# Four weight products of a two-block transformer kernel turned around: residual with tokens on partitions, activations stationary, 512 weight columns moving

## The chip, the cores and the metric

The kernel runs on one core of one Trainium2 chip. The metric is the device time of one execution in microseconds (us). A core has a matmul engine (PE in the rows, its weight loads PEld), a vector engine (DVE), a scalar engine (ACT), GpSimd (POOL), and DMA queues, here issued from SyncE (SP), ScalarE and GpSimd. Matmul results land in PSUM, which has eight banks of 512 float32 columns on 128 partitions.

## What is computed

256 tokens of 2048 channels go through two blocks, all in float32.

```python
# first block
h = rmsnorm(x, attn_norm)
proj = h @ w_in                      # 2048 x 5376: queries, keys, values of branches a, b, c
mix = concat(rmsnorm(out_a), rmsnorm(out_b), rmsnorm(out_c))   # three kinds of attention
x = x + mix @ w_out                  # 2048 x 2048, "output"
h = rmsnorm(x, ffn_norm)
u = causal_dwconv(h @ w_up)          # 2048 x 11264
x = x + (silu(gate) * up) @ w_down   # 5632 x 2048, "down"
# second block
h = x @ w_in_2                       # branches a, b, c, m and g_merge, 4 x 2048 "gate" columns
gates = sigmoid(g_merge)
merged = sum(gates[b] * (o[b] @ w_branch[b]) for b in range(4))   # 4 x (1024 x 2048), "branch"
y = merged @ w_out_2
x = layer_norm(ALPHA * x + y)
```

## The kernel before

The weights, over 400 MB, pass once through the core. `run` (L429) works through one list of transfers, `stream`, each of 128 partitions by up to 2048 float32 columns (1 MB). Three buffers `raw` are filled from the SP queue; a buffer is filled again when the transfer three places earlier has been converted. Each transfer is used in parts of up to 1024 columns. A part is converted into two float32r tiles whose sum is exact: `h` by the scalar engine (L464), `l` by the vector engine (L478), some two parts ahead of their use. Each operand of a large product is split so, and three of the four partial products are made.

Two functions turn parts into matmuls. `t_tile` (L351) makes one tile of 128 output channels by 256 tokens: for every 128 rows of weights the 128 x 128 block `h` is loaded and the activations, high and low part side by side (512 columns), stream past it (`mm3`, L326), then `l` is loaded and the 256 high columns stream (L327). Both halves of the PSUM bank are then added: `join` (L337) by a copy (L332) and an add (L341), or `add_ps` by two adds into the residual (L347, L348). `n_group` (L375) makes 256 tokens by 512 output channels: the activations of 128 tokens are loaded and 512 weight columns stream past them, three times for each token half (L394 to L396), into two banks, one for each half.

PSUM is handed out by tags: `acc` has three banks, `sc` and `tr` two each, `po` one. `sc`, `tr` and `po` serve attention and transposes.

After each part `step` runs background work, written as generators: attention pairs, norms, splits. `need` runs steps until a result is there. So all engines' instructions stand in one order that Python fixes; each engine works off its own in that order.

The residual is `xT`, channels on partitions: 16 tiles of 128 x 256. `half1` and `half2` (L1126, L1137) add the output projection's two halves to it; `half2` multiplies the second with the norm of branch c, scales and splits for the up products (L1142 to L1165), and sums squares on GpSimd (L753, L754). `down_post` (L1248) adds the down products and splits. `gen_xn` (L1849) transposes the residual for the last step with 32 transposes (L1854). `gate_post` and `br_post` (L1865, L1873) make sigmoid and the merge tile by tile (L1879 to L1882, adds on GpSimd), into `xT`; `gen_ms` splits it. `z_post` and `gen_out` make the layer norm with tokens on partitions.

Order of the stream: memory keys and values, branches a, b, c, output (32 half tiles), up (34 tiles), down block 0, up (32), down block 1 (13 tiles), up (22), the rest of down, then the second block's projections, its gate and branch tiles in turns, and the last product.

Of the kernel before, what the change touches and what calls it, by code (L numbers as in the profile page):

```python
# [9 lines left out]
F32 = mybir.dt.float32  # L10
# [14 lines left out]
# columns of the packed per-channel parameters  # L25
# [9 lines left out]
# columns of the packed one-hot rows and bias tables  # L35
# [67 lines left out]
def _layout(a):  # L103
# [11 lines left out]
    r["wo"] = _lay_t(a["w_out"][0])  # L115
# [3 lines left out]
    for i, n in enumerate(FBLK):  # L119
        r[f"wd{i}"] = _lay_t(wd[f * 128:(f + n) * 128])  # L120
        f += n
# [8 lines left out]
    for n in ("u", "ga", "xb", "gb", "q", "kc", "vc", "ks", "kw", "gc", "qm", "gm", "gg"):  # L130
        r["w2" + n] = _lay_t(o[n])
    r["w2v"] = _lay_n(o["v"])
# [6 lines left out]
    t = [_lay_t(wb[i]) for i in range(4)]  # L139
    r["wbr"] = np.stack([np.concatenate([t[0], t[1]], 2), np.concatenate([t[2], t[3]], 2)], 1)  # L140
# [44 lines left out]
class Build:  # L185
# [5 lines left out]
    def __init__(self, tc, D, out, ctx, taps=None):  # L191
# [28 lines left out]
        self.alone = False  # L220

    # ---- allocation
# [4 lines left out]
    def take(self, i, dt):  # L227
        """half of a two-slot tile; a tile of its own for each use of both halves"""
# [60 lines left out]

    def sm(self):  # L290
# [19 lines left out]
    # ---- small instruction helpers  # L310
# [6 lines left out]
    def split(self, t, dst):  # L317
        """float32 tile -> exact sum of two float32r tiles"""
# [4 lines left out]
    def mm3(self, ps, wh, wl, x, first, last):  # L323
        """ps[:, :T] + ps[:, T:] += w^T x with both operands split; w stationary"""
# [12 lines left out]
    def join(self, ps, scale=None):  # L337
        """the two halves of a product, added"""
# [36 lines left out]
    def n_group(self, ap, xs, post):  # L375
        """out[tokens, 512] for one 512-column group; ap [nl, 128, 2048]"""
# [26 lines left out]
    def add(self, loads):  # L403
        """transfers in order, each followed by the uses of its parts"""
# [102 lines left out]
    # ---- background work  # L507
# [21 lines left out]
    def later(self, *fs):  # L529
        """one function per step, the first in this step"""  # L530
# [17 lines left out]
    def need(self, cond, what):  # L548
        """emit background work until cond() holds"""
# [16 lines left out]

    def head_norm(self, ps, gain, dest, done):
        """per-head (64 partitions) rmsnorm of a projected tile"""
# [22 lines left out]
    def bias_tile(self, dram, row, off=0):  # L591
        """tile[p, j] = f[row][p + j]; read backwards along j it is the bias of keys against queries"""
# [5 lines left out]
    def qk(self, q, k):  # L598
        """scores of two heads: [:, 0:256] second query block, [:, 256:384] first query block"""
# [9 lines left out]
    def key_pair(self):  # L609
        """keys of two heads for 128-row products, the other head's rows zero"""  # L610
# [5 lines left out]
    def key_swap(self, lo, hi, ka, kb):  # L616
        """lo holds a head in its low rows, hi another in its high rows: each into the other half too"""
# [3 lines left out]
    def to_pt(self, P1, P0):  # L621
        """P [query, key] of two heads -> transposed: key block 0 per head [128, 256], key block 1 both heads"""
# [13 lines left out]
    def pv(self, po, pt, v, first, last=True):  # L636
        """po[64 per head, T] += v^T P^T; v(hh, block) -> [128, 64]"""
# [8 lines left out]
    def softmax_a(self, s, bias, P1, P0, sm, sink=None):  # L646
        """P = exp(s + bias - max); sm columns (block, head): 0:4 minus max, 4:8 denominators"""
# [32 lines left out]
    def soft_pair(self, q, k, v, bias_src, rows, done, sink=None, sinkn=None):  # L680
        """two heads of causal softmax attention with a bias by distance; the output replaces q"""
# [75 lines left out]
    def pipe(self, n, *fs):  # L757
        """steps of a software pipeline: stage j handles item i at step i + j"""
# [6 lines left out]
    def group_norm(self, tiles, sq, g0, ys):  # L765
        """rmsnorm over a group's channels, result split into ys"""
# [23 lines left out]
    # ---- the kernel  # L790
    def setup(self):
# [4 lines left out]
        self.xT = self.cp.tile([128, 16, T], F32, name="xT")  # L796
        nc.scalar.preload_act_table_set("natural_log_exp_and_others")
# [5 lines left out]
        # work for the array until the data is here, so that its clock is up by then  # L803
# [16 lines left out]
    def tables(self):  # L820
        """distance -> bias, per head, to DRAM"""
# [64 lines left out]
    def lazy(self, lst, n, what, then=None):  # L886
        """sequence that asks for its n items when first used"""
# [9 lines left out]
    def block1(self):  # L897
        nc, D = self.nc, self.D
        V, A, G = nc.vector, nc.scalar, nc.gpsimd
        # memory keys and values  # L900
# [56 lines left out]
        # branch A  # L957
# [23 lines left out]
        def c_done(o, j):  # L981
            """group C: split with the gain, the common factor comes after the product"""
            g = self.col("gmix", 8 + j)

            def f():
# [6 lines left out]
                def f2():  # L992
# [5 lines left out]
                    def f3():  # L998
                        self.free(o)
                        if j == 7:  # L1000
                            st["rsc"] = self.slot()
                            self.rms_factor(st["sqc"], 1024, st["rsc"], self.epsc)
# [47 lines left out]
        # branches B and C  # L1050
# [54 lines left out]
        def cq_post(j):  # L1105
# [14 lines left out]
            return f  # L1120
        for j in range(8):
# [3 lines left out]
        # output projection, first the A and B halves  # L1125
        def half1(i):  # L1126
            def f(ps):
                if i == 0:
# [5 lines left out]
        sq = {}  # L1134
# [953 lines left out]
```

## Time and profile before

| | us |
|---|---|
| median of 3 runs | 2452.63 |
| lowest, highest | 2452.2, 2453.0 |
| profiled execution, span | 2453.6 |

| engine | busy us | share |
|---|---|---|
| PE | 2426.6 | 99% |
| PEld | 2096.4 | 85% |
| DVE | 1667.2 | 68% |
| ACT | 1323.6 | 54% |
| POOL | 421.6 | 17% |

The page of the profile gives busy times, the chain of work that ended last, and the costliest groups of instructions by line of the kernel. Times of single stages come from windows: the busy time of each engine between two moments, counted from the span's start, with the number of instructions that touch the window.

### The profile page before, as it was taken

Reading aid. Unit: us, or ns where it says so; the run is one execution under the profiler, and the core shown is the slowest. Engines: PE = TensorE matmul, PEld = TensorE weight load, DVE = VectorE, ACT = ScalarE, POOL = GpSimd, SP = SyncE. Lnnn points to the kernel's source line nnn. Section 1 sums busy time; section 2 is a strip of 40 time slices with the busy share of each in tenths; the row PEclk is TensorE's granted clock in tenths of the full one; section 3 lists DMA queues with packets and bytes.
Section 4 is the critical chain, followed back from the end, with each engine's and each line's share of the span. In section 5 each row is a group of like instructions: output and inputs, shape, how many; then the busy total and the mean of one; then the engine's idle time right before and its main releaser. Section 6 shows DMA issues by size and latency. Waiting matters only on the chain.

```text
span 2453.6 us, 35661 instructions
## 1 busy us (share of the span) xinstructions
PE 2426.6 (99%) x13768; PEld 2096.4 (85%) x13768; DVE 1667.2 (68%) x2662; ACT 1323.6 (54%) x2255; POOL 421.6 (17%) x470
## 2 busy tenths in 40 slices
PE   9999999999999999999999999999999999999997
PEld 8887888888888888888888888888888888888887
DVE  6768677877766777577777865757655555555566
ACT  5566566465544554455456645765554444444443
POOL 2113222532200221022003420101001111111101
PEclk9999999999999999999999999999999999999999
DMA  7554544545555555555555555445545555555553
GB/s 287 191 173 139 176 162 145 186 179 198 186 193 185 194 187 190 183 180 192 192 199 171 176 191 185 150 145 188 190 172 189 182 191 183 184 189 189 189 220 124
DMA packets 74295, 449.16 MB, mean 183 GB/s; under 512 B 8734, under 2 KB 14952, under 8 KB 25484
## 3 DMA queue, kind: packets, MB, share of 16 engines
q1 hardware_dynamic: 65052, 433.86, 50.3%
q10 hardware_dynamic: 7040, 6.29, 1.0%
q0 software_dynamic: 2032, 6.72, 0.9%
q8 instruction: 108, 1.77, 0.3%
q14 instruction: 63, 0.52, 0.1%
HBM read 442.97 MB, written 2.17 MB: 181 GB/s over the span
## 4 chain that ended last, share of the span: by engine, by line
PE 93%; DVE 4%; ACT 1%; DMA 1%; POOL 1%; issue 0%; ACTq 0%; DVEq 0%; SPq 0%; POOLq 0%
PE acc L326 51%; PE acc L327 26%; PE acc L394 3%; PE acc L396 3%; PE acc L395 3%; DVE l L478 1%; PE sc L604 1%; DVE s L315 1%; PE po L642 1%; ACT s L312 1%; PE sc L605 1%; DMA raw<-in_wmv_dram 1%; POOL s L754 0%; DMA raw<-in_wu_dram 0%; PE po L1738 0%
## 5 line engine op out<-in xcount | busy, mean ns | idle before, releaser
L326 PE MATMUL acc<-s,h 128*128 128x512 f32 x5680 | 2010.1, 398 | 2.7 <-ACT h L464 1.5
L327 PE MATMUL acc<-s,l 128*128 128x256 f32 x5680 | 1596.1, 281 | 5.0 <-DVE l L478 4.8
L326 PEld LDWEIGHTS acc<-s,h 128*128 128x128 f32 x5680 | 1067.8, 188 | 255.9 <-issue 5.2
L478 DVE TENSOR_TENSOR l<-raw,h 128x1024 fp32r<-128x1024 f32 (+1 forms) x808 | 1003.5, 1251 | 148.6 <-PE acc L327 54.6
L327 PEld LDWEIGHTS acc<-s,l 128*128 128x128 f32 x5680 | 1075.2, 189 | 10.3 <-DVE l L478 9.8
L464 ACT CAST h<-raw 128x1024 fp32r<-128x1024 f32 (+1 forms) x808 | 839.0, 1040 | 368.9 <-PE acc L326 163.5
L341 DVE TENSOR_TENSOR s<-acc,s 128x256 f32<-128x256 f32 x311 | 131.9, 424 | 397.0 <-ACT s L332 396.9
L332 ACT COPY s<-acc 128x256 f32<-128x256 f32 x319 | 118.8, 372 | 439.8 <-PE acc L327 439.8
L1882 POOL TENSOR_TENSOR xT<-xT,s 128x256 f32<-128x256 f32 x48 | 75.4, 1571 | 599.6 <-DVE s L1881 599.6
L1192 POOL TENSOR_TENSOR s<-s,s 128x256 f32<-128x256 f32 x88 | 81.9, 931 | 509.0 <-DVE s L341 509.0
L312 ACT ACTIVATE s<-s 128x256 f32<-128x256 f32 (+1 forms) x251 | 98.8, 413 | 82.8 <-DVE s L341 45.0
L394 PE MATMUL acc<-h,s 128*128 128x512 f32 x352 | 140.7, 400 | 0.9 <-ACT s L320 0.8
L396 PE MATMUL acc<-h,s 128*128 128x512 f32 x352 | 137.5, 391 | 0.2 <-DVE s L321 0.2
L395 PE MATMUL acc<-l,s 128*128 128x512 f32 x352 | 137.3, 390 | 0.0
L312 ACT ACTIVATE s<-s,sm 128x256 f32<-128x256 f32 (+1 forms) x168 | 74.3, 464 | 27.0 <-DVE sm L674 13.6
L315 DVE SCALAR_TENSOR_TENSOR s<-s,cols 128x254 f32<-128x254 f32 (+2 forms) x128 | 80.2, 627 | 6.4 <-ACT s L312 4.0
L312 ACT ACTIVATE s<-s,cols 128x256 f32<-128x256 f32 (+1 forms) x104 | 61.3, 589 | 37.2 <-POOL s L1192 23.9
L394 PEld LDWEIGHTS acc<-h,s 128*128 128x128 f32 x352 | 66.1, 188 | 15.8 <-issue 1.9
L396 PEld LDWEIGHTS acc<-h,s 128*128 128x128 f32 x352 | 66.1, 188 | 15.1 <-DVE s L321 0.7
L395 PEld LDWEIGHTS acc<-l,s 128*128 128x128 f32 x352 | 66.2, 188 | 12.8
L347 DVE TENSOR_TENSOR xT<-xT,acc 128x256 f32<-128x256 f32 x64 | 26.9, 421 | 64.8 <-PE acc L327 64.6
L315 DVE SCALAR_TENSOR_TENSOR s<-s,cols,s 128x255 f32<-128x255 f32 (+5 forms) x106 | 62.5, 592 | 3.5 <-ACT s L312 2.0
(260 smaller groups left out, 1443.1 us busy)
## 6 DMA issues: line engine op xcount, KB each, us to landing
raw<-in_wu_dram SPq DMA_DIRECT2D x88, 1024.0 KB, 4.8
raw<-in_w2gg_dram SPq DMA_DIRECT2D x64, 1024.0 KB, 4.8
raw<-in_wd_dram SPq DMA_DIRECT2D x32, 1024.0 KB, 4.8
raw<-in_wbr_dram SPq DMA_DIRECT2D x32, 1024.0 KB, 4.8
raw<-in_wc_dram SPq DMA_DIRECT2D x16, 1024.0 KB, 4.8
raw<-in_wo_dram SPq DMA_DIRECT2D x32, 512.0 KB, 3.5
raw<-in_wo_dram SPq DMA_DIRECT2D x16, 1024.0 KB, 4.8
raw<-in_wd_dram SPq DMA_DIRECT2D x16, 768.0 KB, 4.2
```

The costliest lines, as they stand in the source:

```text
L312: return self.nc.scalar.activation(out, in_, f, bias=bias, scale=scale, **k)
L315: return (eng or self.nc.vector).scalar_tensor_tensor(out, a, s, b, op0=o0, op1=o1)
L326: m(ps, lhsT=wh, rhs=x.both, start=first, stop=last, skip_group_check=True)
L327: m(ps[:, :T], lhsT=wl, rhs=x[0], start=False, stop=last, skip_group_check=True)
L332: self.nc.scalar.copy(t, ps[:, T:])
L341: self.nc.vector.tensor_add(t, ps[:, :T], t)
L394: m(ps, lhsT=xh[:, ts], rhs=h[:, s], start=k == 0, stop=False)
L395: m(ps, lhsT=xh[:, ts], rhs=l[:, s], start=False, stop=False)
L396: m(ps, lhsT=xl[:, ts], rhs=h[:, s], start=False, stop=k == nl * 4 - 1)
L464: self.nc.scalar.copy(h[:, :b - a], raws[i][:, a:b])
L478: self.nc.vector.tensor_sub(l[:, :n], raws[i][:, a:b], hl[k][:, :n].bitcast(F32))
L1192: G.tensor_mul(u, u, rs[0])
```

## The change

The residual `R` lies with tokens on partitions, in the same memory as `xT`: `res(t, a, b)` is token half t, channels a to b. Output, down, gate and branch products use `n_group` with weights laid out for it; their tiles of 128 channels become groups of 512. For down, gates, branches and the last product `banks` takes two `sc` and two `acc` banks in turn; the output projection keeps `acc`. Where the next product needs channels on partitions, `turn` makes four transposes of 128 columns, after which the scalar engine makes the high and the vector engine the low part. The residual's input is loaded once more in the new layout during branch c. The norm of branch c becomes a scalar per token. `gen_xn` goes; of the gate and branch groups the last two gates stand ahead of the last two branches.

```diff
+    def banks(self):
+        self.alt = not self.alt
+        return [self.sc(), self.sc()] if self.alt else [self.acc(), self.acc()]
+    def res(self, t, a, b):
+        return self.R[:, t * 2048 + a:t * 2048 + b]
+    def turn(self, src, post):
+        p = self.tr()
+        for c in range(2):
+            for t in range(2):
+                self.nc.tensor.transpose(p[:, c * T + t * 128:c * T + t * 128 + 128], src(t, c), self.colr("ident"))
+        return [post(c, p[:, c * T:c * T + T]) for c in range(2)]
...
-    def n_group(self, ap, xs, post):
+    def n_group(self, ap, xs, post, banks=None):
...
-                        st["ps"] = [self.acc(), self.acc()]
+                        st["ps"] = banks() if banks else [self.acc(), self.acc()]
...
+        def r_load():
+            for i in range(2):
+                nc.sync.dma_start(self.R[:, i * 2048:(i + 1) * 2048], D["xr"][:, i * 2048:(i + 1) * 2048])
+        self.hooks[len(self.stream) + 3] = r_load
...
-                self.add_ps(self.xT[:, i], ps)
+                for t in range(2):
+                    x = self.res(t, cg * 512, cg * 512 + 512)
+                    V.tensor_add(x, x, pss[t])
...
+        def half2(cg):
+            def f(pss):
                 self.need(lambda: "rsc" in st, "mix c norm")
+                junk = self.pair(F32)
+                for t in range(2):
+                    x = self.res(t, cg * 512, cg * 512 + 512)
+                    self.stt(x, pss[t], st["rsc"][:, 2 * t:2 * t + 1], x, ALU.mult, ALU.add)
+                    self.act(junk.both, x, AF.Square, accum_out=ss[:, t, cg:cg + 1])
+                self.free(*junk)
+                self.fast.append(gen_x1(cg))
...
+        def gen_x1(cg):
+            yield
+            for jj in range(2):
...
+                ps = self.turn(lambda t, c: self.res(t, (i0 + c) * 128, (i0 + c) * 128 + 128), high)
+                for c in range(2):
+                    self.stt(ys[c][1], ps[c], self.col("gffn", i0 + c), ys[c][0].bitcast(F32), ALU.mult, ALU.subtract)
+                    self.xs2.append(ys[c])
+                yield
...
-        for i in range(0, 16):
-            self.add(self.t_tile(D["wo"][i][:, :1024], YAB(), half1(i)))
+        for cg in range(4):
+            self.add(self.n_group(D["wo"][cg, :2], YAB(), half1(cg)))
...
+        def down_post(b, cg, f0, n):
+            def post(pss):
+                for t in range(2):
+                    x = self.res(t, cg * 512, cg * 512 + 512)
+                    V.tensor_add(x, x, pss[t])
                 if b == 2:
+                    self.fast.append(gen_x2(cg))
...
+            for cg in range(lo, hi):
+                self.add(self.n_group(D[f"wd{b}"][cg], Acts(f0), down_post(b, cg, f0, FBLK[b]), self.banks))
         pairs(0, 17, True)
-        down(0, 0, 16)
+        down(0, 0, 4)
         pairs(17, 33)
-        down(1, 0, 13)
+        down(1, 0, 3)
         pairs(33, 44)
-        down(1, 13, 16)
-        down(2, 0, 16)
+        down(1, 3, 4)
+        down(2, 0, 4)
...
+        def gate_post(b, cg):
+            def post(pss):
+                gt[b] = [self.pair(F32) for _ in range(2)]
                 for t in range(2):
+                    self.act(gt[b][t].both, pss[t], AF.Sigmoid)
...
+        def br_post(b, cg):
+            def post(pss):
+                g = gt.pop(b)
+                if b == 0:
+                    mt[cg] = g
+                for t in range(2):
+                    V.tensor_mul(g[t].both, pss[t], g[t].both)
+                    if b:
+                        (V if (b, cg) == (3, 3) else G).tensor_add(mt[cg][t].both, mt[cg][t].both, g[t].both)
+                        self.free(*g[t])
...
         def gen_ms():
+            for cg in range(4):
+                while cg == 3 and "merged" not in state:
                     yield
...
+                    ps = self.turn(lambda t, c: mt[cg][t].both[:, (2 * jj + c) * 128:(2 * jj + c) * 128 + 128], high)
...
+        for cg in range(4):
+            for b in range(4):
+                if (b, cg) == (2, 3):
+                    gg(2, 3)
+                    gg(3, 3)
+                    br(2, 3)
+                    br(3, 3)
+                elif (b, cg) != (3, 3):
+                    gg(b, cg)
+                    br(b, cg)
         msl = self.lazy(ms, 16, "merged")
         for cg in range(3):
-            self.add(self.n_group(D["wo2"][cg], msl, z_post(cg)))
+            self.add(self.n_group(D["wo2"][cg], msl, z_post(cg), self.banks))
```

## Rows read from the trace of the kernel before

**Rows 1.** Page, parts 1, 2, 4: busy us, granted clock, chain that ended last.

```profile
PE 2426.6 (99%) x13768; PEld 2096.4 (85%) x13768; DVE 1667.2 (68%) x2662; ACT 1323.6 (54%) x2255; POOL 421.6 (17%) x470
...
PEclk9999999999999999999999999999999999999999
...
PE 93%; DVE 4%; ACT 1%; DMA 1%; POOL 1%; issue 0%; ACTq 0%; DVEq 0%; SPq 0%; POOLq 0%
```

**Rows 2.** Page, part 5, costliest groups: busy us, mean ns, idle before, releaser.

```profile
L326 PE MATMUL acc<-s,h 128*128 128x512 f32 x5680 | 2010.1, 398 | 2.7 <-ACT h L464 1.5
...
L478 DVE TENSOR_TENSOR l<-raw,h 128x1024 fp32r<-128x1024 f32 (+1 forms) x808 | 1003.5, 1251 | 148.6 <-PE acc L327 54.6
...
L1882 POOL TENSOR_TENSOR xT<-xT,s 128x256 f32<-128x256 f32 x48 | 75.4, 1571 | 599.6 <-DVE s L1881 599.6
...
L347 DVE TENSOR_TENSOR xT<-xT,acc 128x256 f32<-128x256 f32 x64 | 26.9, 421 | 64.8 <-PE acc L327 64.6
```

**Rows 3.** Windows by stage: length, busy us (count) per engine, clock, DMA share, GB/s.

```profile
278.00:387.20 109.20, 109.20 (x659) 94.71 (x658) 79.01 (x162) 72.45 (x164) 27.61 (x38) 1.00 0.47 159
...
387.20:440.80 53.60, 53.60 (x323) 45.98 (x322) 41.26 (x87) 29.59 (x56) 7.39 (x8) 1.00 0.53 167
440.80:489.00 48.20, 46.84 (x259) 38.95 (x257) 45.28 (x71) 24.27 (x41) 30.55 (x27) 1.00 0.55 183
489.00:682.70 193.70, 191.14 (x1092) 167.91 (x1092) 151.50 (x192) 113.88 (x175) 51.00 (x54) 0.99 0.53 188
...
772.20:949.70 177.50, 177.50 (x1026) 156.51 (x1025) 136.86 (x171) 101.64 (x155) 41.52 (x46) 1.00 0.54 190
...
1803.40:2350.90 547.50, 546.61 (x3106) 474.00 (x3104) 306.29 (x386) 269.86 (x405) 74.64 (x47) 1.00 0.52 185
...
sum 248.60, PE 247.38 PEld 215.46 DVE 156.97 ACT 103.96 POOL 7.15; mean PE 82.46 PEld 71.82 DVE 52.32 ACT 34.65 POOL 2.38
```

**Rows 4.** Windows, same columns, inside the projections and inside the gates.

```profile
1700.00:1800.00 100.00, 100.00 (x579) 88.19 (x578) 62.41 (x91) 55.79 (x91) 0.00 (x0) 1.00 0.54 191
...
1900.00:2300.00 400.00, 400.00 (x2267) 346.90 (x2266) 224.90 (x284) 193.84 (x285) 55.58 (x35) 1.00 0.53 185
```

**Rows 5.** Timeline, PE: start us, duration us. An n_group, then a t_tile.

```profile
80.02 0.39 PE L394 MATMUL acc<-h,s 128*128 128x512 f32 x1
...
101.78 0.39 PE L394 MATMUL acc<-h,s 128*128 128x512 f32 x1
...
102.80 0.40 PE L326 MATMUL acc<-s,h 128*128 128x512 f32 x1
...
104.92 0.40 PE L326 MATMUL acc<-s,h 128*128 128x512 f32 x1
```

**Rows 6.** Timeline, PE: four transposes inside an n_group.

```profile
1468.13 0.39 PE L396 MATMUL acc<-h,s 128*128 128x512 f32 x1
1468.36 0.60 PE L1482 MATMUL tr<-cols,s 128*128 128x128 f32 x4
...
1469.03 0.40 PE L395 MATMUL acc<-l,s 128*128 128x512 f32 x1
...
1471.34 0.39 PE L396 MATMUL acc<-h,s 128*128 128x512 f32 x1
```

**Rows 7.** Timeline, PE: the last product's first group begins, its second begins.

```profile
2350.04 0.28 PE L327 MATMUL acc<-s,l 128*128 128x256 f32 x1
...
2352.43 0.40 PE L394 MATMUL acc<-h,s 128*128 128x512 f32 x1
...
2373.99 0.39 PE L396 MATMUL acc<-h,s 128*128 128x512 f32 x1
...
2375.64 0.39 PE L396 MATMUL acc<-h,s 128*128 128x512 f32 x1
```

**Rows 8.** Waits of PE, 380 to 500 us (total, times, longest); a window therein.

```profile
PE acc L327 <- DVE l L478: 3.9, 9, 2.3
...
494.90:498.00 3.10, 3.04 (x10) 2.67 (x11) 3.03 (x5) 2.18 (x3) 2.20 (x3) 0.53 0.00 0
```

More of the change, by code (lines that the diff above doesn't have):

```diff
@@ L138, in _layout @@
     wb = a["w_branch_2"][0]
-    t = [_lay_t(wb[i]) for i in range(4)]
-    r["wbr"] = np.stack([np.concatenate([t[0], t[1]], 2), np.concatenate([t[2], t[3]], 2)], 1)
+    r["wbr"] = np.stack([_lay_n(wb[i]) for i in range(4)])
     r["wo2"] = _lay_n(a["w_out_2"][0])
@@ L1168, in half2, with high @@
             return f
+        def gen_x1(cg):
+            yield
+            for jj in range(2):
+                i0 = 4 * cg + 2 * jj
+                ys = []
+                def high(c, p):
+                    y = self.pair()
+                    self.act(y[0], p, AF.Copy, scale=self.col("gffn", i0 + c))
+                    ys.append(y)
+                    return p
+                ps = self.turn(lambda t, c: self.res(t, (i0 + c) * 128, (i0 + c) * 128 + 128), high)
[3 more added lines that the diff above has]
+                yield
+            if cg == 3:
+                dg = self.slot()
+                V.tensor_reduce(ss2, ss, AX.X, ALU.add)
+                for t in range(2):
+                    V.tensor_scalar(dg[:, t * 128:t * 128 + 128], self.colr("ident"), ss2[:, t:t + 1], None, op0=ALU.mult)
+                yield
+                r = self.slot()
+                self.rms_rows(dg, 2048, r, self.epsc)
+                self.free(dg)
+                rs[0] = r
@@ L1175, in __getitem__ @@
                 return l[j]
-        for i in range(0, 16):
-            self.add(self.t_tile(D["wo"][i][:, :1024], YAB(), half1(i)))
+        for cg in range(4):
+            self.add(self.n_group(D["wo"][cg, :2], YAB(), half1(cg)))
         ycl = self.lazy(yc, 8, "yc")
-        for i in range(16):
-            self.add(self.t_tile(D["wo"][i][:, 1024:], ycl, half2(i)))
+        for cg in range(4):
+            self.add(self.n_group(D["wo"][cg, 2:], ycl, half2(cg)))
         xs2 = self.lazy(self.xs2, 16, "xs2")
@@ L1889, in post, with high @@
                             self.free(*y)
[L1890 to L1891 removed]
+                    for n in ("lng", "lnb"):
+                        state[n] = row_bcast(D[n], 2048)
             return post
         def gen_ms():
[L1895 to L1904 removed]
+            for cg in range(4):
+                while cg == 3 and "merged" not in state:
+                    yield
+                if cg == 3:
+                    yield
+                for jj in range(2):
+                    ys = []
+                    def high(c, p):
+                        y = self.pair()
+                        A.copy(y[0], p)
+                        ys.append(y)
+                        return p
+                    ps = self.turn(lambda t, c: mt[cg][t].both[:, (2 * jj + c) * 128:(2 * jj + c) * 128 + 128], high)
+                    for c in range(2):
+                        V.tensor_sub(ys[c][1], ps[c], ys[c][0].bitcast(F32))
+                        ms.append(ys[c])
+                    yield
+                for g in mt.pop(cg):
+                    self.free(*g)
         fst = self.cp.tile([128, 2, 8, 6], F32, name="fst")
@@ L1909, in z_tile @@
         def z_tile(j, t, ps):
-            z = xn[t, j]
-            V.tensor_add(z, ps, z)
+            z = self.res(t, j * T, j * T + T)
+            self.stt(z, z, ALPHA, ps, ALU.mult, ALU.add)
             V.bn_stats(fst[:, t, j, :], z)
@@ L1985, in block2, with gg, br @@
                 self.add(self.t_tile(D["w2" + nmn][j], x2, g_post(b, src, j)))
-        def start_xn(h, l):
-            self.slow.append(gen_xn())
-        self.start_xn = start_xn
-        first = True
-        for i in range(16):
-            for b in (0, 1, 2, 3):
-                ld = self.t_tile(D["w2gg"][16 * b + i], x2, gate_post(b, i))
-                if first:
-                    a, e, use = ld[0][1][0]
-                    def use2(h, l, use=use):
-                        self.slow.append(gen_xn())
-                        use(h, l)
-                    ld[0][1][0] = (a, e, use2)
-                    first = False
-                self.add(ld)
-                if b % 2:
-                    subs = []
-                    for k in range(2):
-                        bb = b - 1 + k
-                        xs = self.BR(self, os_[bb], bb)
-                        s = self.t_tile(D["wbr"][i, b // 2][:, k * 1024:(k + 1) * 1024], xs, br_post(bb, i))
-                        (_, [(x0, x1, u)]), = s
-                        subs.append((k * 1024, k * 1024 + 1024, u))
-                    self.add([(D["wbr"][i, b // 2], subs)])
+        def gg(b, cg):
+            self.add(self.n_group(D["w2gg"][4 * b + cg], x2, gate_post(b, cg), self.banks))
+        def br(b, cg):
+            self.add(self.n_group(D["wbr"][b, cg], self.BR(self, os_[b], b), br_post(b, cg), self.banks))
+        for cg in range(4):
+            for b in range(4):
[7 more added lines that the diff above has]
+                    br(b, cg)
         msl = self.lazy(ms, 16, "merged")
         for cg in range(3):
-            self.add(self.n_group(D["wo2"][cg], msl, z_post(cg)))
+            self.add(self.n_group(D["wo2"][cg], msl, z_post(cg), self.banks))
         kept = []
```

153 lines of the change are left out of this document (54 added, 99 removed).

## The prediction

> **What bounds the kernel now.** The page's busy shares come first: the matmul engine is busy in 2426.6 of 2453.6 us, at a granted clock of full speed in every slice, and the chain that ended last runs over it for 93% [rows 1]. Vector and scalar engine have a third and nearly half of the span free. So the time is the matmul stream's, and the question is what one weight block of 128 x 128 costs there. The costliest groups and a stretch of the matmul engine's timeline [rows 2, 5] show the two ways in which the kernel multiplies today. t_tile (L326, L327) holds a weight block and streams the activations past it: 512 columns, then 256. n_group (L394 to L396) holds activations and streams weights: per 128 rows of weights six matmuls of 512 columns for four blocks. Both move 768 columns per block, so by columns they are equal. Durations don't tell them apart (a row's 398 ns overlaps the next matmul); the spacing of starts does.
>
> In windows where only t_tile ran [rows 4], 100 us hold 579 matmuls at one place and 400 us hold 2267 at another: 345.4 and 352.9 ns per pair, thus per block. The stream has two rhythms and stays in one until something disturbs it. n_group's starts [rows 5] go from 80.02 to 101.78 us in 96 steps: 226.7 ns per matmul, or 1.5 x 226.7 = 340.0 ns per block. When a t_tile stream follows an n_group directly, it takes the slow rhythm: 102.80 to 104.92 us are six pairs, 353 ns [rows 5].
>
> **The change, part by part**, against the profiled execution (span 2453.6 us; the median of the runs is 1.0 us lower).
>
> *Matmul rate.* 2496 of the 5680 t_tile blocks become n_group's: output 256, down 44 x 16 = 704, gates and branches 1024 + 512. Their stages now take 53.6 + 48.2, 248.6 and 547.5 us [rows 3]. At 340.0 ns they would be 87.0, 239.4 and 522.2. Of the 101.8 of the output projection about 8.6 are attention matmuls, which stay (53.6 less 128 blocks at about 351 ns). I split the rest into rate (256 x 11, 704 x 12 and 1536 x 13.3 ns: 2.8 + 8.4 + 20.5 = 31.7 us) and other time that goes: about 3.3 of stalls in the second half of the output projection (48.2 less 128 x 351 ns), 0.8 in down, and 4.8 in the gates, where the 32 transposes of gen_xn sit. Together -40.6.
>
> *Stalls at stage edges.* Around 490 us the matmul engine waits 3.9 us for the converted weights of L478, once for 2.3 us, and the granted clock then is 0.53, nearly all at the lower of its two levels, 1.2 GHz, for 3 us [rows 8]. The reason is in the window 440.8 to 489: the vector engine is busy 45.28 of 48.20 us, as each block column costs it a join, a product, an add and a split beside L478 [rows 3]. The change replaces these by one operation on 512 columns per token half and column group, and transposes the result. So the first up stage, 193.7 us for 544 blocks, or 188.5 at the fast rhythm, loses 4.6 of its excess. At the last n_group, from 2350.04 to 2352.43, four matmuls take 2.4 us instead of 0.8, waiting for the last merge and split [rows 7]; the change puts eight sub-tiles of work between them. That is -1.6, and two changes of group there cost 0.3 each less with alternating banks.
>
> *Transposes added.* turn is called 8 times after each of output projection, down and merge, 24 in all, each with four 128-column transposes. Four such in an n_group stretch: twelve steps from 1468.13 to 1471.34 us take 3.21 instead of 2.72, so 0.49 each [rows 6]; 24 x 0.49 = +11.8. This counts the disturbance behind them.
>
> *Group changes.* In the last stage a new group follows from 2373.99 to 2375.64 in six steps, 1.65 instead of 1.36, for it must wait for an eviction with three accumulators and two per group: 0.3 us [rows 7]. The eight groups of the output projection keep these banks: +2.1 for seven changes. In down, gates and branches two pairs of banks alternate; a group's eviction then has a whole group, 10 to 22 us, and costs nothing. Its cover gone, 44 x 0.3 = 13 us. Entering an n_group and attention work inside one add about 1.0.
>
> *Rhythm.* The second up stage runs 177.5 us for 512 blocks, the fast rhythm [rows 3]. Behind an n_group with nothing to disturb it, I expect the slow one: 512 x 6.4 ns = +3.3. The first up stage begins among transposes; I take half of 544 x 6.4 ns, +1.7. The third is slow already.
>
> *Evictions.* An operation on 512 columns lies between the 0.42 us of L347 for 256 and the 1.25 of L478 for 1024 [rows 2]; two per group of 10.9 or 21.8 us, instead of a join each 2.8 or 5.6 us: less work than before. The merge's adds on GpSimd take 1.57 us for 256 columns [rows 2], so up to 3.1 for 512, 6.3 per branch group, beside 33 us of stream.
>
> *DMAs.* Bytes of weights are the same; the output projection's transfers grow from 512 KB to 1 MB, which doubles what three buffers hold. r_load puts 2 MB on SP's queue ahead of attention weights. There the DMA engines are busy 0.47 at 159 GB/s [rows 3]: at the rest, some 180 GB/s, 2.1 MB take 12 us, and three buffers hold 3 x 6.8 us (109.2 for 16 tiles). Nothing then; up to 6 us if the buffers were short when it is issued.
>
> *New waits.* turn's transposes wait for the residual add or the merge and stand in the matmul queue in front of the next products; the copies and splits behind them must be there before the next stage asks for its last rows. Background work is emitted once per 1024 weight columns, 2.7 us, and the last four rows of eight or sixteen come into use three such steps later. Per stage edge this costs between 0 and the 2.3 us of [rows 8], and not below 0; there are three such edges. I take 2.0 in all, nearer the free end, as the vector engine is no longer full there.
>
> The sum: -40.6 - 4.6 - 1.6 - 0.6 + 11.8 + 2.1 + 1.0 + 3.3 + 1.7 + 2.0 = -24.9. Span 2428.7, median about 2427.7, which I round to 2427.5.
>
> **The rivals.**
> - *The weight stream doesn't settle* (slower). Behind each disturbance the n_group matmuls are 231 ns apart on average for ten steps (1469.03 to 1471.34 us, [rows 6]) before they settle at 226.7. If the longer groups held a slower rhythm, as t_tile does for 400 us [rows 4], at 235 ns per matmul a block would cost the 353 ns of today and the whole 31.7 us of rate would be lost: -24.9 + 31.7 = +6.8, 2459.5. It decides at 24.9 us / 2496 / 1.5 = 6.7 ns, so from 233.3 ns per matmul on. Against it: 96 steps in a row at 226.7.
> - *Columns alone count* (no change). If both ways cost the same per column and the spacing seen were an accident of place, rate and rhythm terms go: -24.9 + 31.7 - 5.0 = +1.8, about 2454.5. Against it: the two fast figures, 345.4 and 340.0, come from undisturbed stretches. The Trainium skill has this rule (TensorE: Matmul & The Clock Gate, "Back-to-back issue gap": the isolated gap at full clock is columns / 2.4 plus 2.5 ns); an estimate by it is 325.0 against 323.7 ns per block, so some 3 us of gain in rate, less than the transposes cost. By that rule the change brings about nothing. The trace doesn't agree: 226.7 ns stand here for its 215.8.
> - *Group changes wait after all*: two banks are finished at once, and a sigmoid of both queues behind a conversion on the scalar engine. At the 0.3 us of [rows 7] for 44 groups +13, 2441.
> - *Stage edges stall*: where turn feeds the up stage, the second block and the last product, each costs what the first up stage lost now, 193.7 - 188.5 = 5.2; three of them and the 4.6 not gained, less my 2.0: +18, 2446.
> - That the change isn't what it says: the number of n_group matmuls must rise by 1.5 x 2496 = 3744. The diff leaves no doubt, so it has no chance of its own.
>
> **How the numbers follow.** Forecast 70%, with a range of its own from 2417 (both up stages fast, no waits: -5.0 - 2.0 - 3.1) to 2437 (the half of each unknown cost more). Not settling 6%, columns alone 6%, group changes 10%, stage edges 8%. The range to be right 8 times in 10 reaches from 2416 to 2446, over the forecast and the two cases of waits. About 0.2%, 4.9 us, is what a measurement here can tell from no change. Faster by more: the forecast, group changes, and half of the stage edges, 84%. Within: the other half and most of columns alone, 9%. Slower: 7%.
>
> **What would show it.** In the trace after, steps of 226.7 ns inside gate groups, a gate and branch stage near 527 us instead of 547.5, down near 244 in sum, the second up stage at 181 instead of 177.5, and no clock below full speed near 490 us. I am wrong if the steps inside long groups are 230 ns or more, if a group's first matmul waits in down or gates, or if the transposes wait for what they turn.

## The result

The changed kernel takes 2424.48 us in the median of four runs (2423.99 to 2426.03), the kernel before, timed beside it, 2452.41 (2451.93 to 2453.0): a ratio of 0.9891, 95% interval 0.9872 to 0.9910. Forecast were 2427.5 and a range of 2416 to 2446. The profiled execution has a span of 2422.8 us instead of 2453.6, so 30.8 us less; the stages are compared in these two executions.

The page of the changed kernel, parts 1 and 5 (busy us, mean ns, idle before, releaser; L345 and L346 are t_tile's matmuls now, L413 to L415 n_group's, L497 and L483 the conversions):

```profile
PE 2401.7 (99%) x12588; PEld 2037.8 (84%) x12588; DVE 1587.2 (66%) x2363; ACT 1271.9 (52%) x2071; POOL 351.4 (15%) x419
...
L497 DVE TENSOR_TENSOR l<-raw,h 128x1024 fp32r<-128x1024 f32 x800 | 1016.0, 1280 | 381.7 <-PE sc L414 193.0
...
L345 PE MATMUL acc<-s,h 128*128 128x512 f32 x3184 | 1130.3, 399 | 0.9 <-DVE s L340 0.9
...
L413 PE MATMUL acc<-h,s 128*128 128x512 f32 x864 | 341.6, 395 | 0.0
...
L413 PE MATMUL sc<-h,s 128*128 128x512 f32 x736 | 287.2, 390 | 0.0
...
L1929 POOL TENSOR_TENSOR s<-s,s 128x512 f32<-128x512 f32 x22 | 39.0, 1793 | 604.2 <-DVE s L1927 604.2
```

The pairs of L345 and L346 went from 5680 to 3184, by 2496. As in [rows 1], the matmul engine is busy from end to end, so nearly all of the gain has to be in the stream itself. The windows of the changed kernel, with the columns of [rows 3], in the order output, first, second and third up stage, the second block's projections, gates and branches, last product, tail; the last line is the sum of the three down stages:

```profile
386.40:485.30 98.90, 98.90 (x477) 80.99 (x476) 63.73 (x100) 53.87 (x96) 7.38 (x8) 1.00 0.50 175
485.30:675.40 190.10, 190.10 (x1102) 166.34 (x1101) 147.47 (x189) 113.24 (x177) 44.80 (x49) 1.00 0.54 189
762.40:943.30 180.90, 180.90 (x1025) 156.86 (x1024) 136.99 (x171) 101.56 (x155) 40.54 (x46) 1.00 0.53 186
1008.70:1133.00 124.30, 124.30 (x705) 107.80 (x704) 93.05 (x116) 69.28 (x105) 27.48 (x31) 1.00 0.53 186
1223.00:1794.80 571.80, 569.99 (x3316) 492.45 (x3316) 395.86 (x778) 337.98 (x643) 87.63 (x126) 1.00 0.51 176
1794.80:2320.40 525.60, 525.60 (x2332) 435.13 (x2332) 277.27 (x239) 225.67 (x241) 43.26 (x30) 1.00 0.55 194
2320.40:2386.20 65.80, 65.80 (x296) 54.48 (x295) 38.98 (x55) 30.23 (x48) 0.00 (x0) 1.00 0.62 228
2386.20:2422.80 36.60, 23.65 (x193) 23.06 (x191) 28.17 (x69) 5.22 (x14) 7.83 (x10) 0.87 0.16 58
...
sum 242.40, PE 242.40 PEld 200.58 DVE 135.22 ACT 101.19 POOL 7.12; mean PE 80.80 PEld 66.86 DVE 45.07 ACT 33.73 POOL 2.37
```

| stage | before | after | difference | terms of the forecast |
|---|---|---|---|---|
| up to the output product | 387.2 | 386.4 | -0.8 | 0 |
| output | 101.8 | 98.9 | -2.9 | -0.3 |
| first up stage | 193.7 | 190.1 | -3.6 | -1.9 |
| down, three stages | 248.6 | 242.4 | -6.2 | -6.3 |
| second up stage | 177.5 | 180.9 | +3.4 | +3.3 |
| third up stage | 124.3 | 124.3 | 0.0 | 0 |
| second block's projections | 570.3 | 571.8 | +1.5 | +1.0 |
| gates and branches | 547.5 | 525.6 | -21.9 | -22.4 |
| last product | 66.3 | 65.8 | -0.5 | -1.2 |
| tail | 36.4 | 36.6 | +0.2 | 0 |

(The terms are the prediction's, each turn's 0.49 us put where it lies, two of eight behind the stage that it closes, and 0.8 of the 1.0 for entries with the output. The 2.0 of new waits and the other 0.2 stood for no one stage.)

In the gates the steps between the starts of n_group's matmuls are those of [rows 5], also across a change of banks (from `acc` to `sc`). Timeline of the changed kernel, matmul engine (start us, duration us), 92 steps in 20.85 us, 226.6 ns each:

```profile
1850.10 0.39 PE L414 MATMUL acc<-l,s 128*128 128x512 f32 x1
...
1870.95 0.39 PE L413 MATMUL sc<-h,s 128*128 128x512 f32 x1
```

Why is a block cheaper so, with the same 768 columns? Where its tail begins, the changed kernel streams 256 columns at a time, 23 steps in 2.75 us, 119.6 ns each:

```profile
2386.17 0.28 PE L2092 MATMUL acc<-s,s 128*128 128x256 f32 x1
...
2388.92 0.28 PE L2094 MATMUL acc<-s,s 128*128 128x256 f32 x1
```

An estimate from these two steady figures: 256 columns more cost 107.0 ns, which leaves 12.6 ns of each matmul that don't go by columns. n_group makes 1.5 matmuls per block and t_tile two; half of 12.6 ns is 6.3, and 346.5 - 340.0 is 6.5. So the number of matmuls is enough to explain the difference from the fast rhythm, whichever operand is held. No run here holds the weights with equal lengths throughout or varies the number alone, so this is not shown. The slow rhythm's further 6.5 ns are the subject of the later experiments.

### The profile page after: what moved, and what is told of

Read it like the earlier page. It is cut to its first block, busy times and chain, and to the rows that moved or that the text cites. A ratio compares the mean times of both kernels' runs of the same rounds, so it can differ in the third digit from the quotient of the medians.

```text
span 2422.8 us, 32877 instructions
## 1 busy us (share of the span) xinstructions
PE 2401.7 (99%) x12588; PEld 2037.8 (84%) x12588; DVE 1587.2 (66%) x2363; ACT 1271.9 (52%) x2071; POOL 351.4 (15%) x419
## 4 chain that ended last, share of the span: by engine, by line
PE 94%; DVE 2%; ACT 1%; POOL 1%; DMA 1%; issue 0%; SPq 0%; ACTq 0%; DVEq 0%; POOLq 0%
PE acc L345 28%; PE acc L346 14%; PE acc L413 8%; PE acc L415 8%; PE acc L414 8%; PE sc L415 7%; PE sc L413 7%; PE sc L414 7%; PE sc L632 1%; PE po L670 1%; DVE l L497 1%; PE sc L633 1%; DMA raw<-in_wmv_dram 1%; ACT s L331 1%; PE tr L306 0%; DVE s L1390 0%
## 5 line engine op out<-in xcount | busy, mean ns | idle before, releaser
L497 DVE TENSOR_TENSOR l<-raw,h 128x1024 fp32r<-128x1024 f32 x800 | 1016.0, 1280 | 381.7 <-PE sc L414 193.0
L483 ACT CAST h<-raw 128x1024 fp32r<-128x1024 f32 x800 | 839.6, 1050 | 560.4 <-PE sc L415 244.1
L345 PE MATMUL acc<-s,h 128*128 128x512 f32 x3184 | 1130.3, 399 | 0.9 <-DVE s L340 0.9
L346 PE MATMUL acc<-s,l 128*128 128x256 f32 x3184 | 892.3, 280 | 2.0 <-DVE l L497 1.8
L345 PEld LDWEIGHTS acc<-s,h 128*128 128x128 f32 x3184 | 598.3, 188 | 143.4 <-issue 2.9
L346 PEld LDWEIGHTS acc<-s,l 128*128 128x128 f32 x3184 | 601.5, 189 | 4.6 <-DVE l L497 4.0
L413 PE MATMUL acc<-h,s 128*128 128x512 f32 x864 | 341.6, 395 | 0.0
L415 PE MATMUL acc<-h,s 128*128 128x512 f32 x864 | 336.9, 390 | 0.0
L413 PE MATMUL sc<-h,s 128*128 128x512 f32 x736 | 287.2, 390 | 0.0
L415 PE MATMUL sc<-h,s 128*128 128x512 f32 x736 | 286.5, 389 | 0.0
L414 PE MATMUL sc<-l,s 128*128 128x512 f32 x736 | 286.4, 389 | 0.0
L415 PEld LDWEIGHTS acc<-h,s 128*128 128x128 f32 x864 | 162.1, 188 | 34.8
L413 PEld LDWEIGHTS acc<-h,s 128*128 128x128 f32 x864 | 162.2, 188 | 34.0 <-issue 1.6
L415 PEld LDWEIGHTS sc<-h,s 128*128 128x128 f32 x736 | 138.1, 188 | 28.9
L413 PEld LDWEIGHTS sc<-h,s 128*128 128x128 f32 x736 | 138.2, 188 | 28.5
```

The lines of the kernel that those rows point to most:

```text
L345: m(ps, lhsT=wh, rhs=x.both, start=first, stop=last, skip_group_check=True)
L346: m(ps[:, :T], lhsT=wl, rhs=x[0], start=False, stop=last, skip_group_check=True)
L413: m(ps, lhsT=xh[:, ts], rhs=h[:, s], start=k == 0, stop=False)
L414: m(ps, lhsT=xh[:, ts], rhs=l[:, s], start=False, stop=False)
L415: m(ps, lhsT=xl[:, ts], rhs=h[:, s], start=False, stop=k == nl * 4 - 1)
L483: self.nc.scalar.copy(h[:, :b - a], raws[i][:, a:b])
```

## The experiments

Every difference below is against the changed kernel unless it says otherwise. 2424.48 us is its time, 2422.8 its span.

**Only the gates by t_tile again.** Is the gain one of rate, or of what lies beside the stream?

```diff
+                r, g = self.right(ps), gt[b][i // 2][i % 2]
+                V.tensor_add(g, ps[:, :T], r)
...
+                self.act(g, g, AF.Sigmoid)
...
-            self.add(self.n_group(D["w2gg"][4 * b + cg], x2, gate_post(b, cg), self.banks))
+            for i in range(4):
+                self.add(self.t_tile(D["w2gg"][4 * b + cg, i], x2, gate_post(b, cg, i)))
```

> The changed kernel, with only the 16 gate groups made by t_tile again (64 tiles of 128 columns, same transfers and bytes; the columns then mean other channels, so the numbers of the gates are not the reference's). Theory, the cost per block depends on which operand is held: 1024 blocks go from 340 ns to 353 (slow rhythm) or 346 (fast rhythm), so the gate and branch stage grows from 525.6 us by 13.3 or 5.5 us, and the time from 2424.5 to 2430 to 2438. Rival, columns alone count and the gain came from evictions and transposes: the stage stays within 2 us of 525.6.

It took 2437.03 us, 12.6 more. Below are the window of the gate and branch stage, 538.6 us instead of 525.6, in which 1024 blocks are t_tile's now, and the timeline inside a gate group: from 1830.13 to 1849.21 us are 54 pairs at 353.3 ns.

```profile
1793.80:2332.40 538.60, 538.60 (x2843) 460.28 (x2842) 295.54 (x302) 251.15 (x336) 43.17 (x30) 1.00 0.54 189
```

```profile
1830.13 0.40 PE L345 MATMUL acc<-s,h 128*128 128x512 f32 x1
...
1849.21 0.40 PE L345 MATMUL acc<-s,h 128*128 128x512 f32 x1
```

The matmul engine is busy in all of both stages, the DMA share is 0.54 and 0.55, and no other engine is full: the 13.0 us are the rate, 13.3 by the slow rhythm. "Columns alone count" falls.

**Three banks everywhere.** What do alternating banks save?

```diff
-        return [self.sc(), self.sc()] if self.alt else [self.acc(), self.acc()]
+        return [self.acc(), self.acc()]
```

> The changed kernel, with the three acc banks for every group instead of two pairs of banks in turn. Theory of the prediction, a change of group with three banks costs 0.3 us: 44 changes, +13 us, 2437. Rival, from the output stage of the changed kernel, whose changes with three banks show no wait: the cost depends on how soon the first bank's reader is done; down and branches (one operation of some 0.7 us on that bank) cost nothing, gates (a sigmoid) at most 0.3 us for 16 groups, so 2424 to 2430.

2424.97 us, the same. The gate and branch stage takes 525.2 us:

```profile
1794.90:2320.10 525.20, 525.20 (x2331) 434.89 (x2330) 276.92 (x238) 225.41 (x240) 43.26 (x30) 1.00 0.55 194
```

So a change of group is free there too, and the 0.3 us of [rows 7] are no price of the three banks as such. With three banks the next group needs the first bank of the last one only at its fourth matmul, 0.68 us later. Where one operation reads that bank, it is free by then. In the last product several operations read it one after the other, and there this run has the wait again at both changes, once from 2343.27 us on: two steps take 0.72 us instead of 0.45. With four banks the changed kernel has none.

```profile
2343.27 0.39 PE L415 MATMUL acc<-h,s 128*128 128x512 f32 x1
2343.68 0.47 PE L413 MATMUL acc<-h,s 128*128 128x512 f32 x1
2343.99 0.39 PE L414 MATMUL acc<-l,s 128*128 128x512 f32 x1
```

That the reader's length makes the difference is argued from these places; it was not varied by itself.

**Each turn's transposes twice.**

```diff
-        for c in range(2):
+        for c in [0, 1, 0, 1]:
             for t in range(2):
```

> The changed kernel, with each turn's four transposes made twice. Theory, transposes lie fully on the matmul engine's path: 24 x 4 x 0.109 us = +10.4 us, 2435; the disturbance behind them is not doubled. Rival, part of them fills time that the matmul engine would wait anyway: +0 to +5 us.

2434.93 us, 10.45 more for 96 transposes: 0.109 us each. Of four, with the disturbance behind them, [rows 6] show 0.49, so the 24 turns cost the kernel close to the 11.8 us of the sum. Timeline of this run, one turn of eight transposes, 0.79 us to the next product, where four take 0.36 in the changed kernel (below it):

```profile
2303.83 1.04 PE L306 MATMUL tr<-cols,s 128*128 128x128 f32 x8
2304.62 0.47 PE L413 MATMUL sc<-h,s 128*128 128x512 f32 x1
```

```profile
2295.28 0.60 PE L306 MATMUL tr<-cols,s 128*128 128x128 f32 x4
2295.64 0.48 PE L413 MATMUL sc<-h,s 128*128 128x512 f32 x1
```

**The kernel before, with less work for the vector engine around 490 us.**

```diff
-                V.tensor_mul(t, t, st["rsc"])
...
-                    self.square_into(sq[0], x, i == 0)
+                    if i == 0:
+                        G.memset(sq[0], 1.0)
```

> The kernel before, where the second half of the output projection leaves out the product with the norm of branch c on the vector engine (L1142) and the squares on GpSimd (L753, L754); what comes out is not the reference's. Theory, the wait of 3.9 us near 490 us comes from a full vector engine: per tile 0.5 us of L1142 go and L478 falls from 1.55 to about 1.25 us, so the wait falls under 1 us, the granted clock stays at full speed, and the span falls by 5 to 8 us to about 2447. Rival, the weights of the up products come late because the 512 KB transfers before them fill only half of the buffers: the wait stays within 1 us of 3.9, the span above 2451.

The wait is gone: the trace names none of the matmul engine between 380 and 500 us. The second half of the output product takes 44.4 us, the first up stage 189.0, where [rows 3] have 48.2 and 193.7: 8.5 us less, at full clock. This is one execution against one. In the two more executions that follow, the two stretches take 239.8 and 239.7 us, with 3.0 us of this wait and the clock at full speed, so against them it is 6.4 and 6.3 less: the fall of the clock near 490 us belonged to the first profile alone.

```profile
439.70:484.10 44.40, 44.40 (x259) 38.81 (x258) 36.05 (x61) 26.09 (x44) 0.00 (x0) 1.00 0.64 213
484.10:673.10 189.00, 189.00 (x1092) 166.57 (x1091) 147.24 (x186) 111.94 (x172) 44.90 (x49) 1.00 0.54 190
```

So the full vector engine, with GpSimd's squares beside it, made the wait, and not the 512 KB transfers, which are still there. How much the product and how much GpSimd's squares do to it was not taken apart. The span, 2443.6, is 10.0 less than in the first profile, but the stages behind came out in other rhythms, which leads to the next runs.

**Two more executions of the kernel before.** Timed beside the experiments, it took between 2445.7 and 2458.1 us at one clock (0.997 to 0.999), while the runs of no variant of the changed kernel with t_tile as it is lay more than 2.1 us apart.

> The kernel before, unchanged, profiled again: other executions of it ran between 2446 and 2458 us at the same clock, those of the changed kernel within 2 us. Theory, the rhythm of t_tile's stream is set by chance at the wait near 490 us and kept through the undisturbed stages behind it: the stages from 489 to 1278 us and the gates come out at 346.5 or 353 ns per block, and the stages' differences add up to the difference of the spans. Rival, the spread lies in waits (attention, edge of stages) and every stage's steady spacing is as in the first profile.

> As the run before, one more execution of the kernel before; same two theories.

The second and third up stage, in the first of these runs and then in the second:

```profile
771.00:951.90 180.90, 180.90 (x1027) 156.95 (x1026) 136.76 (x171) 101.59 (x155) 41.45 (x46) 1.00 0.53 186
1026.10:1150.50 124.40, 124.40 (x707) 107.84 (x706) 93.06 (x116) 69.29 (x105) 27.61 (x31) 1.00 0.52 186
```

```profile
770.30:951.20 180.90, 180.90 (x1027) 156.96 (x1025) 136.72 (x171) 101.54 (x155) 41.36 (x46) 1.00 0.53 186
1024.10:1146.20 122.10, 122.10 (x707) 106.76 (x706) 93.08 (x116) 69.23 (x105) 27.60 (x31) 1.00 0.54 189
```

The first profile has 177.5 [rows 3] and 124.3:

```profile
1024.00:1148.30 124.30, 124.30 (x706) 107.76 (x705) 93.05 (x116) 69.29 (x105) 27.60 (x31) 1.00 0.52 186
```

So the same stage, with the same instructions and no wait, is fast in one execution and slow in another; three executions show three combinations. Spans were 2456.0, 2450.3 and 2453.6. In these two stages the rhythm is chance in the kernel before and not a property of the stage. That does not hold everywhere: the first up stage is fast behind 500 us in all three, and the gates and branches are slow in all three (2267, 2266 and 2266 matmuls between 1900 and 2300 us). Not all of the spread was traced to the rhythm: the wait near 490 us differs too (the first up stage takes 191.1 us in both runs from its first to its last block, instead of 193.4).

**Disturbing the slow rhythm.** In the changed kernel the first up stage is fast from its norm factor's two float32 matmuls at 497.43 us on, the second and third are slow throughout. Can such a disturbance make them fast? Two kernels put two kinds of disturbance 16 blocks into the two stages (four transposes, or two float32 matmuls, which show as four rows), and a third has the two matmuls deeper inside both. The first kernel:

```diff
+        def knock_mm():
+            p = self.tr()
+            for i in range(2):
+                nc.tensor.matmul(p[:, i * 128:i * 128 + 128], lhsT=self.ones, rhs=self.ones, start=True, stop=True)
+        def knock_tr():
+            p = self.tr()
+            for i in range(4):
+                nc.tensor.transpose(p[:, i * 128:i * 128 + 128], self.ones, self.colr("ident"))
...
+        self.when[len(self.subs) + 1] = knock_mm
         pairs(17, 33)
...
+        self.when[len(self.subs) + 1] = knock_tr
```

> The changed kernel with two small additions on the matmul engine behind the second part of an up stage: two float32 matmuls of 128 columns ahead of the second up stage, four float32 transposes ahead of the third. Theory, t_tile's rhythm is set by the kind of what disturbs it last, and float32 matmuls (as behind the norm factor in the first up stage) leave it fast, transposes slow: second up stage 180.9 to about 178 us, third 124.3 to about 124.7; time 2422. Rival, it depends on the moment and not on the kind: either stage may come out fast (178, 122.5) or slow (181.3, 124.7). Second rival, the rhythm belongs to the stage's data and places: both stay slow, 181.3 and 124.7.

> As the run before, the two additions changed over: transposes ahead of the second up stage, float32 matmuls ahead of the third. Theory by kind: second 181.3, third about 122.5 us, time 2423. Rivals: by the moment, either; by data and places, both slow (181.3 and 124.7), time 2425.

> The changed kernel with two float32 matmuls of 128 columns behind the 9th block of the second up stage (where the slow rhythm is at its longest step, 241 ns) and behind the 8th block of the third (233 ns). In the runs before, the disturbances came after the step of 236 ns and left the stream slow; in the first up stage they came after 241 and left it fast. Theory, the step at which the disturbance comes decides: the second up stage goes from 180.9 to about 178 us; the third, at 233, to 122.5 or stays at 124.7; time 2419.5 to 2422. Rival, the rhythm doesn't depend on the step: 181.3 and 124.7, time 2425.

2424.89, 2424.81 and 2426.19 us; in all three runs the second stage takes 181.3 and the third 124.8. In the slow rhythm the step from a 512-column matmul to its 256-column one is 233, 241 and 236 ns in turn. The six additions came at four places, three of them behind the step of 236 ns and one behind that of 241, and neither kind nor place helped. In the third kernel they came behind the 9th and 8th part, so the 72nd and 64th block, and not where the expectation put them; the 72nd follows a step of 241 ns, the 64th one of 236, and 233 was not tried. In the first up stage the same kind behind the same step of 241 ns left the stream fast, so these two alone don't decide. The timeline of the third kernel (L353 and L354 are t_tile there): behind the disturbance the spacing is that of before, 353 ns from 788.81 to 789.87 us.

```profile
787.90 0.28 PE L354 MATMUL acc<-s,l 128*128 128x256 f32 x1
788.02 0.60 PE L230 MATMUL tr<-ones 128*128 128x128 f32 x4
788.38 0.48 PE L353 MATMUL acc<-s,h 128*128 128x512 f32 x1
...
788.81 0.40 PE L353 MATMUL acc<-s,h 128*128 128x512 f32 x1
...
789.87 0.40 PE L353 MATMUL acc<-s,h 128*128 128x512 f32 x1
```

A longer disturbance does move the stream, in the traces at hand. In the second block's projections two float32 matmuls of 256 columns (four rows, 1.02 us) come eight times, eight blocks apart. From one to the next the changed kernel takes 3.64, 3.68, 3.64, 3.64, 3.68, 3.64 and 3.64 us. The two longer stretches have the slow rhythm's step of 241 ns, the others none above 233 past their first block: so this disturbance makes fast stretches slow, and each slow one fast. The three executions of the kernel before show the same, behind every slow stretch between two of these disturbances.

```profile
1275.39 1.02 PE L1711 MATMUL tr<-s,s 128*128 128x256 f32 x4
1279.07 1.02 PE L1711 MATMUL tr<-s,s 128*128 128x256 f32 x4
1282.71 1.02 PE L1711 MATMUL tr<-s,s 128*128 128x256 f32 x4
```

**Lengths no longer in turns.** n_group always settles, and all its matmuls have 512 columns; t_tile alternates 512 and 256. The next kernels make all high products of a few blocks first and then their low ones (8 blocks, or 2; the edit is that for 2).

```diff
-                    for k in range(c, e):
-                        s = slice((k - c) * 128, (k - c + 1) * 128)
-                        self.mm3(ps, h[:, s], l[:, s], xs[k], k == 0, k == nk - 1)
+                    m = self.nc.tensor.matmul
+                    for k0 in range(c, e, 2):
+                        ks = [(k, slice((k - c) * 128, (k - c + 1) * 128)) for k in range(k0, min(k0 + 2, e))]
+                        for k, s in ks:
+                            m(ps, lhsT=h[:, s], rhs=xs[k].both, start=k == 0, stop=False, skip_group_check=True)
+                        for k, s in ks:
+                            m(ps[:, :T], lhsT=l[:, s], rhs=xs[k][0], start=False, stop=k == nk - 1, skip_group_check=True)
```

> The changed kernel, with the remaining t_tile parts ordered otherwise: the eight high products (512 columns) of a part first, then its eight low products (256 columns). Theory, the slow rhythm comes from 512 and 256 columns taking turns: runs of one length settle, 8 x 226.7 and 8 x 119.8 ns as in the last product, 346.5 per block in every stage, so the second up stage takes 177.5 and the third 122.0 us instead of 180.9 and 124.3, time 2417 to 2420. Rival, the rhythm belongs to weights held and activations moved, whatever the order: 353 ns stay, 2424.5.

> As the run before, in runs of two: two high products, then two low ones. By the theory of turns half as many changes of length: between 346.5 and 350 ns per block, 2419 to 2422. Rival: 353 ns, 2424.5.

2420.51 us with runs of eight, 2418.58 with runs of two. The second and third up stage with runs of two, and then with runs of eight:

```profile
761.60:939.90 178.30, 178.30 (x1025) 155.57 (x1024) 137.02 (x171) 101.47 (x155) 40.65 (x46) 1.00 0.53 189
1005.20:1127.80 122.60, 122.60 (x705) 106.97 (x704) 93.20 (x116) 69.23 (x105) 27.56 (x31) 1.00 0.53 188
```

```profile
763.60:942.30 178.70, 178.70 (x1025) 157.28 (x1024) 136.96 (x171) 99.93 (x155) 40.63 (x46) 1.00 0.53 188
1007.60:1130.50 122.90, 122.90 (x705) 108.13 (x705) 93.19 (x116) 68.17 (x105) 27.54 (x31) 1.00 0.53 187
```

Both stages are out of the slow rhythm: 512 blocks in 178.3 us are 348.2 ns each. The theory's size, 346.5, is not reached, and runs of eight, with a quarter of the changes, are not better than runs of two (349.0). The timeline with runs of two: six blocks from 764.12 to 766.21 us, 348 ns each.

```profile
764.12 0.39 PE L391 MATMUL acc<-s,l 128*128 128x256 f32 x2
764.35 0.63 PE L389 MATMUL acc<-s,h 128*128 128x512 f32 x2
...
766.21 0.40 PE L391 MATMUL acc<-s,l 128*128 128x256 f32 x2
```

Runs of two are the fastest version here: 0.9865 of the kernel before (0.9850 to 0.9879), 5.9 us under the changed kernel's median.

**The same order in the kernel before.** How much of the change is then left?

> The kernel before, with t_tile's parts in runs of two high and two low products and nothing else. Theory: every undisturbed t_tile stage takes 348.4 ns per block in every execution, so the gate and branch stage takes 540 us instead of 547.5, the second up stage 178.4, and the times spread less than the 12 us of the kernel before; about 2440, so that holding the activations is still worth 2496 x 8.4 ns = 21 us of rate. Rival, the gain of this order belongs to the changed kernel's places: 2446 to 2458 as before.

2440.07 us (2439.56 to 2440.81), a ratio of 0.9954 (0.9937 to 0.9970) to the kernel before. The second up stage, and gates and branches:

```profile
768.20:946.60 178.40, 178.40 (x1027) 155.69 (x1026) 136.86 (x171) 101.49 (x155) 41.50 (x46) 1.00 0.53 189
1795.50:2334.70 539.20, 538.89 (x3106) 470.28 (x3104) 307.08 (x385) 269.31 (x403) 74.27 (x47) 1.00 0.53 188
```

Some 12 us come from the order alone, and the four runs lie within 1.3 us. With the same order in both, turning the four products around is worth 2440.1 - 2418.6 = 21.5 us; the two were timed apart, each beside the kernel before (medians 2452.16 and 2451.56).

## Why the prediction was right, and where its terms were off

- *The sum.* The terms as listed add up to -25.5 us, not to the -24.9 that stands there; the -0.6 of the last product's group changes is missing from the total. The span should have been 2428.1 and the median 2427.1, well inside the range.
- *Rate.* Right in kind and size: the gates went back up by 13.0 us when their 1024 blocks went back to t_tile, and gates and branches down by 21.9, of 22.4 forecast. Down: 242.4 us, of which 44 x 4 x 1.36 = 239.4 are the stream and 3.0 six turns.
- *Transposes.* Right: nothing covers them. In the changed kernel the matmul engine waited nowhere for what a turn transposes, nor for its results at the stage edges, so the 2.0 us of *new waits* were too much. The vector engine's busy time in the output stage fell to 63.73 of 98.90 us.
- *Group changes.* Mis-sized: 2.1 us for the output product, measured none. I took the price from the one stage of the trace where the eviction is longer, and put it on stages where one operation frees the bank. The rival "group changes wait after all" falls with the same run. The 1.0 for entries stands on no row and was not measured by itself.
- *Rhythm.* The second up stage's +3.3 came as +3.4, and the second and third up stage, behind an n_group, were slow in every run of the changed kernel that keeps t_tile's order. The +1.7 for the first stage was not paid. But the sum took the rhythms of one execution of before as if they belonged to the kernel. In both further executions the second up stage was already slow, so that the +3.3 came true is luck of the execution that was profiled. The gates, where most of the rate is earned, were slow in all of them.
- *Stalls at stage edges.* Right: a full vector engine, shown in the kernel before. The first up stage gained 3.6. Some 2.2 of it stand against the first profile alone, whose clock fell near 490 us; the two further executions of before don't have that.
- *Evictions and DMAs.* Right to cost nothing: GpSimd's add took 1.79 us for 512 columns, not up to 3.1, and the part up to the output product, with the 2 MB of r_load, took 386.4 us instead of 387.2.
- *What was too much.* The 2.1, 2.0 and 1.7 are 5.8 us, and the span fell by 5.3 more than the listed terms say; the other stages were off by less than 1 us each. Only 3.0 us show in the time, for the profiled execution of before took longer than the median: nearly every time on record is 1.7 us above its span, by which that one took 2455.3 us (an estimate), 2.7 above it. Times of before spread over 12 us with the rhythms and the wait, so that the forecast came within 3 us is in part luck too.
- *Not settling*, the slower rival: inside the gate groups the steps stay at 226.6 ns, and behind a turn they come back to 0.23 us (2295.95 us on).

## What to carry to other kernels

Where the matmul stream bounds a kernel, read the spacing of starts and not durations or columns: here 768 columns per block cost 340 ns in one and a half matmuls of one length, 348 in two that are ordered by length, and 346 to 353 where two lengths take turns. Turning an operand around is worth its transposes when blocks times the difference in spacing is larger (2496 x 12.7 ns against 24 x 0.49 us). And before a stage's time is taken as the kernel's, look at a second execution.

## What the runs showed of the hardware that was not expected

- t_tile's alternating stream has two steady rhythms, 346.5 and 353 ns per block, with no wait, at one clock, and with the same instructions. Which one comes was chance in two stages of the kernel before, and the same in every execution in others. In the second and third up stage of the changed kernel it was the slow one, and six short disturbances didn't change it; a longer one, 1.02 us, made it fast each time that it met the slow one. Why there are two, and what of a disturbance decides, stays open.
- Ordering equal lengths together, even two and two, took the choice away in every stage looked at: 348 ns. Why runs of eight are no better than runs of two stays open as well.
- An n_group with three banks and two per group changes groups without a wait when one operation frees its first bank: 525.2 us against 525.6 with four.
